# First SwiGLU step: the up half's scale taken with the residual; low parts of 54 weight units by VectorE instead of an accumulating DMA

## The chip, the cores and the metric

The kernel runs on one core of one Trainium2 chip. Its engines are TensorE (PE in the profile, with its weight loads as PEld), VectorE (DVE), ScalarE (ACT), GpSimd (POOL) and SyncE (SP, which here only issues DMAs). The metric is the time of one execution on the device in microseconds (us); the trace and the profile page come from one execution taken with the profiler.

## The reference

A two-layer encoder over 512 tokens of width 1024 (the first layer mixes by S5 and gated linear attention, the second by retention), in float32:

```
for i in range(2):
    x = x + 0.5 * swiglu_ffn(rmsnorm(x, ffn1_norm[i]), ffn1_w1[i], ffn1_w2[i])
    h = rmsnorm(x, mix_norm[i])
    x = x + (s5_gla_mixer(h, ...) if i == 0 else retention_mixer(h, ret_w_in, ret_norm, ret_w_out))
    x = x + 0.5 * swiglu_ffn(rmsnorm(x, ffn2_norm[i]), ffn2_w1[i], ffn2_w2[i])
return rmsnorm(x, final_norm)

def rmsnorm(x, g):   return x * rsqrt(mean(x * x, -1) + 1e-6) * g
def swiglu_ffn(h, w1, w2):
    gate, up = split(h @ w1, 2, axis=-1)          # 2816 columns each
    return (silu(gate) * up) @ w2
```

`retention_mixer` projects h to q, k (8 heads of 128), v (8 heads of 256) and a gate, rotates q and k by cosine and sine tables, forms decayed scores per head, multiplies them with v, normalizes each head, multiplies with silu of the gate and projects back.

## The kernel before

The state x lies transposed in SBUF: 8 tiles of 128 features x 512 tokens. Every product of float32 numbers is made of three matmuls: each operand is split into a high part and a low part (the rest), and `mm3` (L194) adds high x high (L196), high x low (L197) and low x high (L198) in one PSUM bank. A matmul here is 128x128 weights with 512 columns. The norm's division by the root mean square is left out of the operands: rs (L170, one value per token, the same in all partitions) multiplies results instead.

**Weight units.** A unit is 128x1024 numbers, 512 KB, and serves 24 matmuls. `weights` (L175) stages it: SP loads `raw` (4 tiles), ScalarE casts the high part `wh` (L183, 3 tiles of each of `wh` and `wl`), and the low part `wl` comes in one of two ways. With `plain`, VectorE subtracts the high part from `raw` (L185). Without it, `lows` lets ScalarE write -raw, rounded, into `wl` (L191), and a DMA from GpSimd's queue accumulates `raw` into it (L192). The weight loads are given a priority AHEAD (50, 150, 50 by stage, L31), by which a scheduler puts their instructions that much earlier than their place in the program; every engine then works off its own queue in order. PSUM has 7 banks `mm` in a ring: a new product takes the bank that was used seven products before, once what read it is done.

**First FFN** (`ffn`, 0 to 421 us). The first product runs over 22 pairs j, a gate unit and an up unit each. `gate` (L231 on) makes, per pair: t = gate x rs (L232), s = silu(t) (ScalarE, L234), u = up x rs (L236), g = u x s (L238), and splits g into high (ScalarE, L223) and low (VectorE, L224). Behind the pairs j = 5 to 12 the S5 preparation is put in: eight blocks of table work, in which VectorE makes `vt` and `wt` (L626 to L628) and the rotation tables (L718 to L723), GpSimd makes its half of `wt` with the same three lines, TensorE transposes `vt` (L649) and multiplies with `wt` (L662), and ScalarE copies the results (L650, L665). The second product runs over 8 output blocks n of 66 matmuls each, its weights in 22 units, and adds 0.5 x the bank to x[n] (L269), from which the next norm's operands are prepared (`prep`).

**Retention** (1370 to about 1800 us). Four groups g of two heads: four units q, k, q, k (`qk`), four value units over four banks (`values`), two scores of four banks each (`scores`), four gate units (`out_gate`), and `attend` per head. In the first group the values come before the scores, in the others after the first head's scores. `rotated` takes a bank with three multiplies (L1083, L1084, L1085; the last frees it) and an addition (L1086); the cosine and sine tables are loaded in the first group after its first unit (L1105) and scaled by rs (L1106, L1107). `scores` multiplies each bank with the decay (L1129). `attend` ends in L1164, L1165 (VectorE), L1167 (ScalarE) and L1168 (VectorE). Between the first FFN and the retention mixer lie the S5 and attention mixer and two FFNs of another form (`ffn7`, seven products in place of eight); after it follow one more of these and the final norm.

Of the kernel before, what the change touches and what calls it, by code (L numbers as in the profile page):

```python
# [20 lines left out]
ALU = mybir.AluOpType  # L21
# [29 lines left out]
def encoder(tc, I, out, dbg=None):  # L51
    nc = tc.nc
    V, A, G, T = nc.vector, nc.scalar, nc.gpsimd, nc.tensor
# [3 lines left out]
    with ExitStack() as ctx:  # L57
# [9 lines left out]
        x = [xs[:, i] for i in range(KT)]  # L67
# [27 lines left out]
        def tmp(tag, shape=(128, S), dt=F32):  # L95
            return tp.tile(list(shape), dt, name=tag, tag=tag)

        def bank(name="mm"):
            return pp.tile([128, S], F32, name=name, tag="mm")
# [46 lines left out]
        def prep(i, n, acc):  # L146
            if n in SEVEN:
                operand7(i, n)
            else:
                operand(i, n)  # L150
            squares(i, acc)
# [9 lines left out]
        def new_acc():  # L161
            return tp.tile([128, S], F32, name="sumsq", tag="sumsq", bufs=1)

        def rstd(acc):
            st = sp.tile([128, S], F32, name="st", tag="st")
            T.matmul(st, ones, acc, start=True, stop=True)
            sd = tmp("tc")
            A.activation(sd, st, AF.Sqrt, bias=eps, scale=1.0 / D)
            rs = tp.tile([128, S], F32, name="rs", tag="rs", bufs=1)
            V.reciprocal(rs, sd)  # L170
            return rs

        phase = [0]

        def weights(src, plain=False):  # L175

            with tc.high_priority(AHEAD[phase[0]]):
                c = slice(0, src.shape[-1])
                raw = wp.tile([128, 1024], F32, name="raw", tag="raw", bufs=4)
                dma(raw[:, c], src)  # L180
                h = wp.tile([128, 1024], F32R, name="wh", tag="wh")
                l = wp.tile([128, 1024], F32R, name="wl", tag="wl")
                A.copy(h[:, c], raw[:, c])  # L183
                if plain:
                    V.tensor_tensor(l[:, c], raw[:, c], f32(h[:, c]), op=ALU.subtract)  # L185
                else:
                    lows(l[:, c], raw[:, c])
            return h, l

        def lows(l, raw):  # L190
            A.activation(l, raw, AF.Copy, scale=-1.0)  # L191
            G.dma_start(l, raw, accum_op=ALU.add)  # L192

        def mm3(ps, lh, ll, rh, rl, first, last, go_on=False):  # L194

            T.matmul(ps, lh, rh, start=first, stop=False, skip_group_check=go_on)  # L196
            T.matmul(ps, lh, rl, start=False, stop=False, skip_group_check=go_on)  # L197
            T.matmul(ps, ll, rh, start=False, stop=last, skip_group_check=go_on)  # L198

        def project(*srcs, loaded=None):  # L200

            w = loaded or [weights(src) for src in srcs]
            res = [bank() for _ in w]
            for k in range(KT):
                c = slice(k * 128, (k + 1) * 128)
                for ps, (h, l) in zip(res, w):
                    mm3(ps, h[:, c], l[:, c], yh[k], yl[k], k == 0, k == KT - 1)
            return res

        def project_tokens(src):  # L210

            banks = [bank() for _ in range(4)]
            for u in range(4):
                h, l = weights(src[u])
                for k2 in range(2):
                    k, c = u * 2 + k2, slice(k2 * 512, (k2 + 1) * 512)
                    for t in range(4):
                        tt = slice(t * 128, (t + 1) * 128)
                        mm3(banks[t], yh[k][:, tt], yl[k][:, tt], h[:, c], l[:, c], k == 0, k == KT - 1)
            return banks  # L220

        def split(src, hi, lo):
            A.copy(hi, src)  # L223
            V.tensor_tensor(lo, src, f32(hi), op=ALU.subtract)  # L224


        def ffn(w1, w2, acc, nxt, slot, filler=None, loaded=None):
            gh, gl = [], []

            def gate(j, pg, pu, rs):  # L230
                t = tmp("ta")  # L231
                V.tensor_tensor(t, pg, rs, op=ALU.mult)  # L232
                s = tmp("tb")
                A.activation(s, t, AF.Silu)  # L234
                u = tmp("tc")
                V.tensor_tensor(u, pu, rs, op=ALU.mult)  # L236
                g = tmp("ta")
                V.tensor_tensor(g, u, s, op=ALU.mult)  # L238
                h, l = slot(2 * j), slot(2 * j + 1)
                split(g, h, l)  # L240
                gh.append(h)
                gl.append(l)

            first = project(w1[0, 0], w1[0, 1], loaded=loaded)
            for j in range(1, NPAIR):
                pg, pu = (project(w1[j, i])[0] for i in range(2))
                if j == 1:
                    rs = rstd(acc)
                    gate(0, *first, rs)
                gate(j, pg, pu, rs)  # L250
                if filler is not None:
                    filler(j)
            acc = new_acc()
            units = {}

            def second(n, k):

                u, i = divmod(n * NPAIR + k, 8)
                if u not in units:
                    units[u] = weights(w2[u])  # L260
                c = slice(i * 128, (i + 1) * 128)
                h, l = units[u]
                return h[:, c], l[:, c]

            for n in range(KT):
                ps = bank()
                for k in range(NPAIR):
                    mm3(ps, *second(n, k), gh[k], gl[k], k == 0, k == NPAIR - 1)
                V.scalar_tensor_tensor(x[n], ps, 0.5, x[n], op0=ALU.mult, op1=ALU.add)  # L269
                prep(n, nxt, acc)  # L270
            return acc

# [469 lines left out]
        def s5_gla(acc, nxt, mp):  # L742
# [5 lines left out]


            ub = project(W[0], W[1])  # L750
            rs = rstd(acc)
            rq, rk = slot("rq"), slot("rk")
# [268 lines left out]
            for ps in project_tokens(I["ab_v"]):  # L1021
                z = ytile(F32)
                A.copy(z, ps)
                v.append(z)
# [51 lines left out]
        def retention(acc, nxt, mp):  # L1076
            slot = lambda name, dt=F32: mp.tile([128, S], dt, name=name, tag="u", bufs=32)
            W = I["ret_in"]
            rs = None

            def rotated(ps, cos, sin):
                m1, m2 = tmp("ta"), tmp("tb")
                V.tensor_tensor(m1, ps, cos, op=ALU.mult)  # L1083
                V.tensor_tensor(m2[0:64], ps[64:128], sin[64:128], op=ALU.mult)  # L1084
                V.tensor_tensor(m2[64:128], ps[0:64], sin[0:64], op=ALU.mult)  # L1085
                V.tensor_tensor(m1, m1, m2, op=ALU.add)  # L1086
                h, l = slot("rh", F32R), slot("rl", F32R)
                split(m1, h, l)
                return h, l
# [5 lines left out]
            def qk(g):  # L1095
                nonlocal rs
                for h2 in range(2):
                    for w in range(2):
                        ps = project(W[g, h2 * 2 + w])[0]
                        if rs is None:  # L1100
                            rs = rstd(acc)

                            for tab, name in ((ctab, "rcos"), (stab, "rsin")):
                                t = tmp("tc")
                                dma(t, I[name])  # L1105
                                V.tensor_tensor(tab[0], t, rs, op=ALU.mult)  # L1106
                                V.tensor_tensor(tab[1], tab[0], rs, op=ALU.mult)  # L1107
                        (q, k)[w][g * 2 + h2] = rotated(ps, ctab[w], stab[w])
# [23 lines left out]
                    pts[h].append((hi, lo))  # L1132

            def out_gate(g, i):
                ps = project(W[g, 8 + i])[0]
                t = tmp("ta")
                V.tensor_tensor(t, ps, rs, op=ALU.mult)
                z = ytile(F32)
                A.activation(z, t, AF.Silu)
                so[g * 4 + i] = z  # L1140
# [96 lines left out]
        with tc.tile_pool(name="g0a", bufs=14) as ga:  # L1237
# [6 lines left out]
            def filler(j):  # L1244
                if j == 1:
                    dma(ident, I["ident"])
                next(pieces, None)
                if j == 12:
                    for _ in pieces:
                        raise RuntimeError("S5 pieces left")  # L1250
                    wk_pool.__exit__(None, None, None)
                    gb.append(ctx2.enter_context(tc.tile_pool(name="g0b", bufs=18)))
# [10 lines left out]
        w2 = lambda i: (I["w2a"][i], I["w2b"][i])  # L1263
# [158 lines left out]
```

## Time and profile before

| | |
|---|---|
| time, median of 3 runs | 2162.1 us (2160.69 to 2163.96) |
| the profiled execution: its time, its span | 2168.18 us, 2166.4 us |
| TensorE busy, mean granted clock | 2091.4 us (97%), 0.988 of full speed |
| VectorE, ScalarE, GpSimd busy | 1384.0 us, 1144.9 us, 308.7 us |
| high parts cast (L183) | 227 of 1026 ns |
| low parts by ScalarE and DMA (L191, L192) | 221 of each |
| low parts by VectorE (L185) | 72, of 128x1024 and 128x768 |

Section 5 of the page groups instructions by line; its last columns tell how long the engine stood just before them and what ended that. A wait is put down to what came last. Matmuls overlap: one is busy 0.39 us and the next starts 0.23 us after it, so a pause shows as idle time in brackets, with its releaser. The granted clock is given as a share of full speed (2.4 GHz; the other level is 1.2).

### The profile page before, as it was taken

How to read it: one execution, taken by the hardware profiler on the slowest of the kernel's cores; microseconds unless marked ns; L12 is line 12 of the kernel's file. 1: busy time of each engine (PE TensorE's matmuls, PEld its weight loads, DVE VectorE, ACT ScalarE, POOL GpSimd, SP SyncE). 2: the span in 40 equal slices, each digit the busy share in tenths (PEclk: the TensorE clock that was granted, in tenths of full speed). 3: DMA queues.
4: the chain of work that ended last, by engine and by line, in shares of the span. 5: the costliest groups of instructions: out<-in, count | busy, mean ns of one | idle time of the engine just before them, and what ended most of it. 6: DMA issues, size and time to landing. Idle time of an engine off the chain costs nothing.

```text
span 2166.4 us, 31101 instructions
## 1 busy us (share of the span) xinstructions
PE 2091.4 (97%) x12088; PEld 1819.0 (84%) x12088; DVE 1384.0 (64%) x2233; ACT 1144.9 (53%) x1696; POOL 308.7 (14%) x330
## 2 busy tenths in 40 slices
PE   8989999998999999999999999999999998999998
PEld 6877788776888999997989898778888888899997
DVE  7798211059939868578868576454535368868574
ACT  7544444364377555456646364455555566454453
POOL 3432112211012000002000001201111112010001
PEclk9999999998999999999999999999999999999999
DMA  8878888885566463544445352757676754354541
GB/s 233 207 191 224 200 189 191 206 230 164 147 157 160 127 157 127 145 137 117 125 139 166 113 149 100 189 153 177 155 184 150 173 143 126 115 152 132 142 141 49
DMA packets 115860, 340.23 MB, mean 157 GB/s; under 512 B 19040, under 2 KB 33760, under 8 KB 115584
## 3 DMA queue, kind: packets, MB, share of 16 engines
q1 hardware_dynamic: 83888, 222.36, 30.5%
q0 software_dynamic: 31824, 115.88, 28.3%
q8 instruction: 95, 1.56, 0.3%
q14 instruction: 53, 0.43, 0.1%
HBM read 208.18 MB, written 14.14 MB: 103 GB/s over the span
## 4 chain that ended last, share of the span: by engine, by line
PE 55%; DVE 11%; DMA 6%; issue 4%; ACT 3%; SPq 1%; POOL 1%; DVEq 0%; POOLq 0%; ACTq 0%
PE mm L196 18%; PE mm L198 18%; PE mm L197 18%; DMA raw<-in_ffn_w_dram 2%; DMA wl<-raw 1%; DVE s L318 1%; DMA raw<-in_w2b_dram 1%; DVE wl L185 1%; DVE s L312 1%; DVE s L317 1%; DVE s L311 1%; ACT r13h L223 1%; SPq L761 1%; DVE r13l L224 0%; DVE st L956 0%
## 5 line engine op out<-in xcount | busy, mean ns | idle before, releaser
L183 ACT CAST wh<-raw 128x1024 fp32r<-128x1024 f32 (+1 forms) x227 | 232.1, 1026 | 369.0 <-issue 204.2
L192 POOL DMA_DIRECT2D wl<-raw x221 | 190.8, 865 | 1593.4 <-ACT wl L191 1227.8
L196 PE MATMUL mm<-y,wh 128*128 128x512 f32 x776 | 309.7, 399 | 8.0 <-ACT wh L1229 5.0
L198 PE MATMUL mm<-y,wl 128*128 128x512 f32 x776 | 306.6, 395 | 8.6 <-DMA wl<-raw 8.6
L197 PE MATMUL mm<-y,wh 128*128 128x512 f32 x776 | 307.8, 397 | 0.1
L196 PE MATMUL mm<-g,wh 128*128 128x512 f32 (+1 forms) x672 | 259.5, 387 | 4.3 <-ACT g L223 4.3
L197 PE MATMUL mm<-g,wh 128*128 128x512 f32 (+1 forms) x672 | 258.9, 385 | 0.2 <-DVE g L224 0.2
L198 PE MATMUL mm<-g,wl 128*128 128x512 f32 (+1 forms) x672 | 258.9, 385 | 0.0
L191 ACT ACTIVATE wl<-raw 128x1024 fp32r<-128x1024 f32 x221 | 233.1, 1055 | 38.7 <-PE mm L197 23.3
L196 PEld LDWEIGHTS mm<-y,wh 128*128 128x128 f32 x776 | 147.2, 190 | 45.4 <-ACT wh L1229 5.0
L198 PEld LDWEIGHTS mm<-y,wl 128*128 128x128 f32 x776 | 147.1, 190 | 44.4 <-DMA wl<-raw 11.1
L197 PEld LDWEIGHTS mm<-y,wh 128*128 128x128 f32 x776 | 147.3, 190 | 34.4 <-DVE y L106 2.5
L196 PEld LDWEIGHTS mm<-g,wh 128*128 128x128 f32 x672 | 126.5, 188 | 29.2 <-ACT g L223 5.2
L198 PEld LDWEIGHTS mm<-g,wl 128*128 128x128 f32 x672 | 126.7, 188 | 25.7
L197 PEld LDWEIGHTS mm<-g,wh 128*128 128x128 f32 x672 | 126.6, 188 | 25.3 <-DVE g L224 1.1
L398 DVE SCALAR_TENSOR_TENSOR ta<-mm,rs 128x512 f32<-128x512 f32 (+1 forms) x74 | 49.8, 674 | 98.9 <-PE mm L198 98.9
L301 ACT CAST wh<-raw 128x1024 fp32r<-128x1024 f32 x66 | 69.2, 1048 | 65.4 <-PE mm L197 49.3
L159 POOL TENSOR_TENSOR sumsq<-sumsq,tb 128x512 f32<-128x512 f32 x47 | 72.1, 1535 | 205.8 <-ACT tb L158 204.7
L346 ACT COPY sv<-mm 128x256 f32<-128x256 f32 x198 | 72.0, 364 | 43.6 <-PE mm L198 43.0
L185 DVE TENSOR_TENSOR wl<-raw,wh 128x1024 fp32r<-128x1024 f32 (+1 forms) x72 | 81.1, 1129 | 14.6 <-ACT wh L183 14.6
L223 ACT CAST r2h<-s 128x512 fp32r<-128x512 f32 x66 | 41.0, 622 | 92.2 <-DVE s L312 92.1
L389 ACT ACTIVATE tb<-ta 128x512 f32<-128x512 f32 x66 | 41.7, 632 | 84.1 <-DVE ta L388 84.1
(391 smaller groups left out, 5576.6 us busy)
## 6 DMA issues: line engine op xcount, KB each, us to landing
wl<-raw POOLq DMA_DIRECT2D x221, 512.0 KB, 5.4
raw<-in_ffn_w_dram SPq DMA_DIRECT2D x196, 512.0 KB, 3.7
raw<-in_w2b_dram SPq DMA_DIRECT2D x48, 512.0 KB, 3.3
raw<-in_ret_in_dram SPq DMA_DIRECT2D x48, 512.0 KB, 3.6
raw<-in_w2a_dram SPq DMA_DIRECT2D x24, 384.0 KB, 3.0
raw<-in_ret_out_dram SPq DMA_DIRECT2D x16, 512.0 KB, 3.8
raw<-in_ab_in_dram SPq DMA_DIRECT2D x13, 512.0 KB, 5.2
wd<-wt SPq DMA_DIRECT2D x16, 256.0 KB, 2.9
```

The lines of the kernel that those rows point to most:

```text
L159: G.tensor_tensor(acc, acc, sq, op=ALU.add)
L183: A.copy(h[:, c], raw[:, c])
L185: V.tensor_tensor(l[:, c], raw[:, c], f32(h[:, c]), op=ALU.subtract)
L191: A.activation(l, raw, AF.Copy, scale=-1.0)
L192: G.dma_start(l, raw, accum_op=ALU.add)
L196: T.matmul(ps, lh, rh, start=first, stop=False, skip_group_check=go_on)
L197: T.matmul(ps, lh, rl, start=False, stop=False, skip_group_check=go_on)
L198: T.matmul(ps, ll, rh, start=False, stop=last, skip_group_check=go_on)
L223: A.copy(hi, src)
L301: A.copy(h, up)
L346: A.copy(z, ps[:, left])
L398: V.scalar_tensor_tensor(m[:, c], ps[:, c], 0.5, rs[:, c], op0=ALU.mult, op1=ALU.mult)
```

## The change

In `gate` the up bank is multiplied with s directly (L236, now in a tile `tc`), and rs is left to the end: the residual becomes two operations, m = bank x 0.5 x rs and x[n] + m. The low part is made by VectorE (`plain`) for the gate units behind j = 13 (8 units), all 22 units of the second product, and in the retention mixer for the k units, every odd value unit and every odd gate unit (8 of each). The q units, the even ones and all units of the first layer's mixer keep the DMA.

```
-        def project(*srcs, loaded=None):
-            w = loaded or [weights(src) for src in srcs]
+        def project(*srcs, loaded=None, plain=False):
+            w = loaded or [weights(src, plain) for src in srcs]
...
-                h, l = weights(src[u])
+                h, l = weights(src[u], phase[0] == 2 and u % 2 == 1)
...
                 s = tmp("tb")
                 A.activation(s, t, AF.Silu)
-                u = tmp("tc")
-                V.tensor_tensor(u, pu, rs, op=ALU.mult)
-                g = tmp("ta")
-                V.tensor_tensor(g, u, s, op=ALU.mult)
+                g = tmp("tc")
+                V.tensor_tensor(g, pu, s, op=ALU.mult)
...
-                pg, pu = (project(w1[j, i])[0] for i in range(2))
+                pg, pu = (project(w1[j, i], plain=j > 13 and i == 0)[0] for i in range(2))
...
-                    units[u] = weights(w2[u])
+                    units[u] = weights(w2[u], True)
...
-                V.scalar_tensor_tensor(x[n], ps, 0.5, x[n], op0=ALU.mult, op1=ALU.add)
+                m = tmp("ta")
+                V.scalar_tensor_tensor(m, ps, 0.5, rs, op0=ALU.mult, op1=ALU.mult)
+                V.tensor_tensor(x[n], x[n], m, op=ALU.add)
...
-                        ps = project(W[g, h2 * 2 + w])[0]
+                        ps = project(W[g, h2 * 2 + w], plain=w == 1)[0]
...
-                ps = project(W[g, 8 + i])[0]
+                ps = project(W[g, 8 + i], plain=i % 2 == 1)[0]
```

The scheduler orders the queues anew, so instructions move that the diff does not name. The numbers behind the names below count buffers; they differ between the two kernels for the same buffer.

GpSimd's queue in the first FFN, early in the S5 preparation; wl_590 of the kernel before and wl_582 of the changed one are the same unit's low part. Before:

```order
L192 DMA wl_494<-raw_491 128x1024
L192 DMA wl_526<-raw_523 128x1024
L192 DMA wl_590<-raw_587 128x1024
L626 TENSOR_TENSOR wa0_180<-pw0_479,par_327 128x576
L627 TENSOR_TENSOR wa1_181<-pw1_480,par_327 128x576
L628 TENSOR_TENSOR wt1_574<-wa0_180,wa1_181 128x576
L626 TENSOR_TENSOR wa0_180<-pw0_479,par_327 128x576
```

The same place now:

```order
L192 DMA wl_488<-raw_485 128x1024
L192 DMA wl_520<-raw_517 128x1024
L626 TENSOR_TENSOR wa0_180<-pw0_473,par_323 128x576
L627 TENSOR_TENSOR wa1_181<-pw1_474,par_323 128x576
L628 TENSOR_TENSOR wt1_566<-wa0_180,wa1_181 128x576
L192 DMA wl_582<-raw_579 128x1024
L626 TENSOR_TENSOR wa0_180<-pw0_473,par_323 128x576
```

The three table operations moved ahead of that unit's DMA.

ScalarE's queue between the seventh and the eighth S5 block (g is the pair's product, vs the block's table). Before:

```order
L183 CAST wh_1847<-raw_1845 128x1024
L191 ACTIVATE wl_1848<-raw_1845 128x1024
L650 COPY vs_1657<-mm_1661 128x4x128
L223 CAST g_1653<-ta_1651 128x512
L650 COPY vs_1657<-mm_1671 128x4x128
```

The same place now:

```order
L183 CAST wh_1821<-raw_1819 128x1024
L191 ACTIVATE wl_1822<-raw_1819 128x1024
L223 CAST g_1629<-tc_1627 128x512
L650 COPY vs_1633<-mm_1637 128x4x128
L650 COPY vs_1633<-mm_1647 128x4x128
```

L223 moved ahead of both copies.

ScalarE's queue at the end of the first group's second head in the retention mixer (oh are its outputs, wh_14040 and wh_13975 the last k unit of the second group, wh_14128 and wh_14062 its first value unit). Before:

```order
L183 CAST wh_14040<-raw_14038 128x1024
L191 ACTIVATE wl_14041<-raw_14038 128x1024
L1167 ACTIVATE oh_13901<-ta_13898,columns_78 128x512
L183 CAST wh_14128<-raw_14126 128x1024
L1167 ACTIVATE oh_13908<-ta_13905,columns_78 128x512
L191 ACTIVATE wl_14129<-raw_14126 128x1024
```

The same place now:

```order
L183 CAST wh_13975<-raw_13973 128x1024
L183 CAST wh_14062<-raw_14060 128x1024
L1167 ACTIVATE oh_13837<-ta_13834,columns_78 128x512
L191 ACTIVATE wl_14063<-raw_14060 128x1024
L1167 ACTIVATE oh_13844<-ta_13841,columns_78 128x512
```

The value unit's cast moved ahead of the first L1167. VectorE's queue a little later, where the second group's rotations end and its first scores are multiplied with the decay. Before:

```order
L1083 TENSOR_TENSOR ta_14070<-mm_14045,y_13253 128x512
L224 TENSOR_TENSOR rl_14035<-ta_14028,rh_14034 128x512
L1084 TENSOR_TENSOR tb_14071<-mm_14045,y_13255 64x512
L1085 TENSOR_TENSOR tb_14071<-mm_14045,y_13255 64x512
L1129 TENSOR_TENSOR tc_14086<-mm_14082,decay_14080 128x512
L1086 TENSOR_TENSOR ta_14070<-ta_14070,tb_14071 128x512
```

The same place now:

```order
L1084 TENSOR_TENSOR tb_14005<-mm_13979,y_13197 64x512
L1085 TENSOR_TENSOR tb_14005<-mm_13979,y_13197 64x512
L224 TENSOR_TENSOR rl_13970<-ta_13963,rh_13969 128x512
L1086 TENSOR_TENSOR ta_14004<-ta_14004,tb_14005 128x512
L185 TENSOR_TENSOR wl_14094<-raw_14091,wh_14093 128x1024
L1129 TENSOR_TENSOR tc_14020<-mm_14016,decay_14014 128x512
```

The first L1129 moved behind L1086 and a new L185.

## Rows read from the trace of the kernel before

**Rows 1.** The page, part 1: busy us, share of the span, instructions.

```profile
PE 2091.4 (97%) x12088; PEld 1819.0 (84%) x12088; DVE 1384.0 (64%) x2233; ACT 1144.9 (53%) x1696; POOL 308.7 (14%) x330
```

**Rows 2.** Busy us by stretch: PE, PEld, DVE, ACT, POOL; clock, DMA share, GB/s.

```profile
100.00:150.00 50.00, 46.62 (x237) 38.37 (x236) 47.10 (x108) 24.03 (x48) 21.39 (x18) 1.00 0.83 214
150.00:200.00 50.00, 42.08 (x206) 34.01 (x205) 47.04 (x62) 20.76 (x44) 14.23 (x11) 0.97 0.69 190
...
250.00:300.00 50.00, 50.00 (x220) 41.02 (x219) 11.76 (x17) 22.71 (x27) 7.74 (x9) 1.00 0.82 191
```

**Rows 3.** TensorE's waits, 0 to 205 us: total, times, longest.

```profile
PE mm L662 <- DVE wt L628: 7.4, 4, 2.3
...
PE mm L649 <- DVE vt L628: 3.9, 3, 1.5
```

**Rows 4.** TensorE's waits, 205 to 420 us.

```profile
PE mm L198 <- DMA wl<-raw: 1.2, 1, 1.2
```

**Rows 5.** TensorE's waits, 1370 to 1480 us.

```profile
PE mm L197 <- DMA wl<-raw: 1.7, 2, 1.1
PE mm L196 <- DVE tb L1085: 0.9, 1, 0.9
```

**Rows 6.** Lines L185 (ns least/median/most, first and last start) and L192, whole execution.

```profile
L185 DVE TENSOR_TENSOR wl<-raw,wh x72: 940/1216/1227, 716.6 to 2137.9; 128x1024 fp32r<-128x1024 f32 x48, 128x768 fp32r<-128x768 f32 x24
...
DMA to landing us min/median/max: 4.4/5.4/9.7
```

**Rows 7.** Timeline of VectorE, S5 blocks: start, us, instruction, idle before.

```profile
188.67 0.68 DVE L236 TENSOR_TENSOR tc<-mm,rs 128x512 f32<-128x512 f32 x1
189.27 0.67 DVE L628 TENSOR_TENSOR vt<-u,u 128x512 f32<-128x512 f32 x1
...
193.67 0.69 DVE L224 TENSOR_TENSOR g<-ta,g 128x512 fp32r<-128x512 f32 x1 [1.91 <-ACT g L223]
```

**Rows 8.** Timeline of ScalarE before the last S5 block.

```profile
192.53 0.59 ACT L650 COPY vs<-mm 128x512 f32<-128x512 f32 x1 [7.29 <-DMA rd<-rot]
```

**Rows 9.** Timeline of GpSimd, early S5 preparation.

```profile
51.92 0.86 POOL L192 DMA_DIRECT2D wl<-raw  x1 [4.64 <-DVE u L601]
...
57.41 1.77 POOL L628 TENSOR_TENSOR wt<-wa,wa 128x576 f32<-128x576 f32 x1
```

**Rows 10.** Timeline of TensorE, first matmuls with two units' low parts.

```profile
61.04 0.39 PE L198 MATMUL mm<-y,wl 128*128 128x512 f32 x1
...
67.62 0.50 PE L198 MATMUL mm<-y,wl 128*128 128x512 f32 x1 [0.92 <-DMA wl<-raw]
```

**Rows 11.** Timeline of VectorE and SP, start of the retention mixer.

```profile
1371.68 3.35 DVE L170 RECIPROCAL rs<-tc 128x512 f32<-128x512 f32 x1 [6.14 <-ACT tc L168]
...
1385.30 0.69 DVE L1106 TENSOR_TENSOR y<-tc,rs 128x512 f32<-128x512 f32 x1 [3.76 <-DMA tc<-in_rsin_dram]
...
1377.02 0.43 SPq L1105 DMA_DIRECT2D tc<-in_rsin_dram  x1
```

**Rows 12.** Timeline of ScalarE, VectorE, TensorE, second group of the retention mixer.

```profile
1462.51 1.05 ACT L183 CAST wh<-raw 128x1024 fp32r<-128x1024 f32 x1 [1.50 <-PE mm L197]
...
1465.00 0.68 DVE L1085 TENSOR_TENSOR tb<-mm,y 64x512 f32<-64x512 f32 x1
...
1473.73 0.69 DVE L1083 TENSOR_TENSOR ta<-mm,y 128x512 f32<-128x512 f32 x1 [0.51 <-PE mm L198]
...
1476.45 0.69 DVE L1129 TENSOR_TENSOR tc<-mm,decay 128x512 f32<-128x512 f32 x1
...
1478.38 0.39 PE L196 MATMUL mm<-wh,y 128*128 128x512 f32 x1
```

**Rows 13.** Third group: VectorE by stretch (span, busy), timelines of VectorE and TensorE.

```profile
1567.50:1582.33 14.83, 12.66 (x20) 1.00 0.75 175
...
1582.33 0.69 DVE L1129 TENSOR_TENSOR tc<-mm,decay 128x512 f32<-128x512 f32 x1
...
1584.85 0.39 PE L196 MATMUL mm<-wh,y 128*128 128x512 f32 x1
```

## The prediction

> **What bounds the kernel now.** I read the page first: TensorE is busy 97% of the span [rows 1], so only its pauses, and stretches at the lower of its two clock levels (2.4 and 1.2 GHz), can be won or added. The table of busy times by stretch comes second: from 250 to 300 us, in the second product of the first FFN, TensorE has no pause and VectorE 38 us of 50 free, while from 100 to 200 us VectorE is busy 47 of 50 and TensorE stands [rows 2]. Third come TensorE's waits: up to 205 us it waits 7.4 + 3.9 = 11.3 us for `wt` and `vt` (L628, VectorE's part of the S5 tables) [rows 3]; at 216.8 us 1.2 us for a low part that comes by DMA [rows 4]; and from 1370 to 1480 us 1.7 us for two such DMAs and 0.9 us for the bank that L1085 frees [rows 5]. The other pauses lie in stages that the change leaves alone.
>
> **The change part by part.** Every row is from the profiled execution, 2168.18 us, which is 6.1 above the median of the three timed runs; I sum against it and carry the sum to the median.
>
> *Low parts by VectorE.* 54 weight units lose one ScalarE operation (L191) and one accumulating DMA (L192) and gain one subtraction (L185), 1.217 us for 128x1024 [rows 6]. The 22 units of the second product and the 8 gate units behind j = 13 fall where TensorE has no pause and VectorE is three quarters idle [rows 2]: 0, and the residual's extra operation too (one of some 0.7 us per output block, after which TensorE works off 66 matmuls of 0.23 us, 15 us, before the next block's result is due). If that cover were gone, it would be 54 x 1.2 = 65 us; nothing in those stages comes near.
>
> *S5 blocks, 112 to 200 us.* VectorE is the late one. In each of the five pairs of this stretch the two products L236 and L238 become one; the next operation starts 0.60 us after L236 (188.67 to 189.27) [rows 7]: 5 x 0.60 = 3.0 us. Before the last block VectorE also stands 1.91 us for ScalarE's L223 [rows 7], which in ScalarE's queue stands behind an L650 that waited 7.29 us for a DMA [rows 8]; now L223 stands ahead of that L650, so 1.9 us go too. TensorE's restart after the last block moves 4.9 us forward. What is late next is TensorE itself, and that only once all 11.3 us are gone. Bounds: 0 (the DMA of the rotation, not VectorE, is last) and -11.3; I take -4.9, since both parts stand in VectorE's own rows.
>
> *A new wait at 61 us.* On GpSimd one L192 now stands behind L626, L627 and L628. Before, it was issued at 51.92, and the last of the three ran until 57.41 + 1.77 = 59.18 [rows 9]. They wait for ScalarE's copies, ahead of which one operation of about 1 us (L191 of the same unit) is gone, so they end at about 58.1. With the landing of 4.4, 5.4 or 9.7 us (least, median, most [rows 6]) the low part is there at 62.5, 63.5 or 67.8; TensorE asks for it at 61.04 [rows 10], and waits 1.5, 2.5 or 6.8. Behind L192 in GpSimd's queue stand the next L626 and L627 and then the next unit's L192; that unit's own pause, 0.92 us at 67.62 [rows 10], goes, since TensorE comes later. Net +0.5, +1.5 or +5.8; I take the median, +1.5. It passes on: the S5 blocks start from TensorE's products.
>
> Here a rule speaks against the change. The granted clock was 1.00 over 100 to 150 us, which hold a pause of 2.3, and 0.97 over 150 to 200, which hold the shorter ones that follow each other closely [rows 2, 3]: 3% of 50 us is 1.5 us of full-speed work lost. The Trainium skill ("TensorE: Matmul & The Clock Gate", Part 1) says that the array falls to 1.2 GHz when it idles and comes back after sustained work. By that the new pause could cost its own length and another 1.5 us. By the row at 145 us a single pause of this length cost no clock; the sum follows the row, the range holds the 1.5.
>
> *The pause at 216.8 us.* This unit's low part still comes by DMA, but the neighbour's transfer of 512 KB goes: between -1.2 (all) and +1 (the same bytes at another moment); I take -0.5.
>
> *Start of the retention mixer.* VectorE waits for the sine table until 1385.30 [rows 11]. Its DMA was issued at 1377.02, behind weight loads on SP's queue that waited for staging tiles held by accumulating DMAs of q and k units. The two k units now free theirs after a subtraction. The tile for the table is free after L170, at 1371.68 + 3.35 = 1375.03 [rows 11], so it can be issued some 2 us sooner and meets fewer transfers (it took 8.3 us). The bank of q0 then comes before TensorE asks, and so do the two late low parts, whose casts stood behind the rotated q: 1.7 + 0.9 [rows 5] and 0.1 for each of three restarts (0.50 in place of 0.39 us [rows 10]) = 2.9. Bounds -2.9 and 0; I take -2.9.
>
> *Retention, second group.* In ScalarE's queue the cast of a value unit, which waits for TensorE until 1462.51, now stands ahead of both L1167; the first of them comes at about 1463.5, after which VectorE has L1168, L1083, L1084 and L1168 again to do, and L1085 starts at 1467.0 instead of 1465.00 [rows 12]: 2.0 late. Ahead of the first L1129 the new L185 (1.1 to 1.2 us) and L1086 (0.6) are put in: 3.75, less 0.51 of idle time in between [rows 12], 3.2. L1129 frees the bank of the first scores for the fourth value bank: before it ended at 1476.45 + 0.69 = 1477.14, and TensorE asked at 1478.38 [rows 12], 1.24 later. So TensorE stands 2.0 us. Groups three and four have the same insertions, but more room: 14.83 - 12.66 = 2.2 us idle in VectorE, and 1584.85 - 1583.02 = 1.8 us [rows 13]: 3.8 - 2.2 - 1.8 = 0. Upper bound: no idle time absorbs anything and two L185 fall in: 2.05 + 2.4 - 1.24 = 3.2 in group two and 2.05 + 2.4 - 1.83 = 2.6 in each of the others, 8.4 in all. Lower bound 0. I take +2.0.
>
> *Sum:* -4.9 + 1.5 - 0.5 - 2.9 + 2.0 = **-4.8 us**: 2163.4 in an execution like the profiled one, **2157.3** at the median.
>
> **The rivals.**
> *More gain:* ScalarE's cast costs the second group nothing, because VectorE's queue has slack that I did not see, and the landing at 61 us is a quick one: -4.8 - 2.0 - 1.0 = -7.8, 2154.3. For it: a third of VectorE's time in these groups is free. Against: each operation named stands in one queue in this order.
> *A gain missing:* the S5 blocks are held by the DMA of the rotation or the sine table stays late, so the change does there not what its queues promise: without the 2.9, -1.9; without the 4.9, +0.1; about 2161. For it: both chains contain a DMA whose landing varies by 2 to 5 us.
> *Slower, by one mechanism:* VectorE's queue in the retention mixer becomes the bound. A subtraction there waits for its cast, which waits for TensorE to leave a weight tile; all behind it, L1085 and L1129 first, free banks late. Price: 8.4 in the three groups, and at the start, where a subtraction stands behind the sine table, the 2.9 is not won: -4.8 + 2.9 - 2.0 + 8.4 = +4.5, 2166.6. It decides from the point where the first L1129 of groups three and four starts more than 1.8 us later against the values' matmuls than before. For it: the same three rows of order in every group. Against: the idle 2.2 us.
> *The clock rule* of the new wait: with a pause of 2.5 us and half clock behind it, -4.8 + 1.5 = -3.3, 2158.8.
>
> **How the numbers follow.** What a measurement can tell from no change is about 0.2%, 4.3 us. The sum 0.42 (its own range 2154.5 to 2160, straddling the 4.3: faster 0.25, same 0.17); more gain 0.20 (faster); a gain missing 0.16 (same); slower 0.15 (0.14 slower, 0.01 same); the clock rule 0.07 (0.02 faster, 0.05 same). Together faster 0.47, same 0.39, slower 0.14. The range reaches from below the second case, 2152, to the slower one, 2166.
>
> **What would show it.** Right: VectorE's pause before the last S5 block gone and TensorE's waits for L628 down from 11.3 to about 6.5; one pause of about 2.5 us at 61 us for a low part; no wait for L1085 at 1388; in the second group one pause of about 2 us, ended by L1129, and none in the next two. Wrong: pauses ended by L1129 in all groups, waits ended by L185, a late sine table, or pauses in the second product, where I count none.

## The result, and the profile after

The changed kernel takes 2154.26 us (median of 6, 2148.64 to 2154.95), the kernel before beside it 2163.37 (6, 2160.69 to 2170.34); the ratio is 0.9942, interval 0.9925 to 0.9958, or -12.5 us (-16.2 to -9.1). The two medians differ by 9.1 us, which is the near end of that interval. The forecast was -4.8: right in sign, and too small by half or more. The profiled execution took 2154.95 us with a span of 2153.0.

The page, part 1, of after answers to [rows 1], and two of its groups show the 54 units that changed hands: L185, 72 before, is now 126 and busy 66.7 us more (147.8 against 81.1; counted: 65). VectorE as a whole has 60.2 us more, since the scale's edit takes 14 shorter operations out on balance.

```profile
PE 2092.0 (97%) x12088; PEld 1820.5 (85%) x12088; DVE 1444.2 (67%) x2273; ACT 1095.6 (51%) x1642; POOL 255.0 (12%) x276
...
L192 POOL DMA_DIRECT2D wl<-raw x167 | 143.5, 859 | 1494.4 <-ACT wl L191 1148.9
...
L185 DVE TENSOR_TENSOR wl<-raw,wh 128x1024 fp32r<-128x1024 f32 (+1 forms) x126 | 147.8, 1175 | 113.1 <-ACT wh L183 108.7
```

The table by stretch [rows 2] says where TensorE gained early on: 150 to 200 us, busy 45.8 us in place of 42.1. In the second product (250 to 300) it is busy throughout, as before, beside a VectorE with 5 us more to do.

```profile
100.00:150.00 50.00, 47.77 (x240) 39.27 (x238) 46.80 (x107) 24.52 (x49) 18.70 (x17) 0.97 0.82 206
150.00:200.00 50.00, 45.78 (x224) 37.51 (x223) 49.00 (x61) 21.15 (x45) 14.46 (x12) 0.97 0.79 218
250.00:300.00 50.00, 50.00 (x220) 41.04 (x219) 16.59 (x20) 17.17 (x21) 2.56 (x3) 1.00 0.52 143
```

TensorE's waits up to 205 us [rows 3]: the 11.3 us for L628 are 5.8, with 0.6 for a cast beside them.

```profile
PE mm L662 <- DVE wt L628: 5.2, 3, 1.9
...
PE mm L649 <- DVE vt L628: 0.6, 1, 0.6
PE mm L649 <- ACT wh L183: 0.6, 1, 0.6
```

VectorE before the last S5 block [rows 7]: the split of `g` (L224) has no idle time in front of it.

```profile
190.05 0.68 DVE L627 TENSOR_TENSOR u<-pv,par 128x512 f32<-128x512 f32 x1
190.66 0.68 DVE L224 TENSOR_TENSOR g<-tc,g 128x512 fp32r<-128x512 f32 x1
```

GpSimd and TensorE around 61 us [rows 9, 10]: L192 stands behind L628 and is issued at 57.91; the low part lands about 5.0 us later, and TensorE waits 1.43.

```profile
56.19 1.77 POOL L628 TENSOR_TENSOR wt<-wa,wa 128x576 f32<-128x576 f32 x1
57.91 0.88 POOL L192 DMA_DIRECT2D wl<-raw  x1
...
62.94 0.50 PE L198 MATMUL mm<-y,wl 128*128 128x512 f32 x1 [1.43 <-DMA wl<-raw]
```

VectorE and SP at the start of the retention mixer [rows 11]: the sine table is issued 3.4 us after the start of the reciprocal, where it was 5.3 (1377.02 against 1371.68).

```profile
1364.04 3.35 DVE L170 RECIPROCAL rs<-tc 128x512 f32<-128x512 f32 x1 [0.78 <-ACT tc L168]
...
1367.42 0.33 SPq L1105 DMA_DIRECT2D tc<-in_rsin_dram  x1
```

Of TensorE's waits from 1350 to 1480 us [rows 5] all that is left is:

```profile
PE mm L196 <- DVE tc L1129: 0.2, 1, 0.2
```

Lined up by the same matmul (its start in the one trace against its start in the other), TensorE is 5.7 us ahead of before at 428 us and gains 3.4 at the start of the retention mixer. It loses about 2.5 between 428 and 1007 us, and gains 2.6 (1007 to 1099 us of before), 0.9 (1293 to 1362) and 4.6 (behind 1480) in FFNs whose code the diff does not touch. Those last three no step of the forecast has; but the 4.6 is no larger than what a second execution of the kernel before gains there by itself (below).

### The profile page after: what moved, and what is told of

Same layout as the page of the kernel before. It is cut to its first block, busy times and chain, and to the rows that moved or that the text cites. A ratio compares the mean times of both kernels' runs of the same rounds, so it can differ in the third digit from the quotient of the medians.

```text
span 2153.0 us, 30985 instructions
## 1 busy us (share of the span) xinstructions
PE 2092.0 (97%) x12088; PEld 1820.5 (85%) x12088; DVE 1444.2 (67%) x2273; ACT 1095.6 (51%) x1642; POOL 255.0 (12%) x276
## 3 DMA queue, kind: packets, MB, share of 16 engines
q8 instruction: 95, 1.56, 0.3%
## 4 chain that ended last, share of the span: by engine, by line
PE 77%; DVE 12%; DMA 4%; ACT 3%; issue 3%; POOL 1%; SPq 0%; DVEq 0%; POOLq 0%; ACTq 0%
PE mm L196 25%; PE mm L198 25%; PE mm L197 25%; DMA raw<-in_ffn_w_dram 2%; DMA wl<-raw 1%; DVE wl L185 1%; POOL sumsq L159 1%; DVE s L318 0%; DVE st L956 0%; PE mm L662 0%; DVE s L312 0%; DMA raw<-in_w2b_dram 0%; DVE st L954 0%; ACT wl L191 0%; DVE s L317 0%
## 5 line engine op out<-in xcount | busy, mean ns | idle before, releaser
L192 POOL DMA_DIRECT2D wl<-raw x167 | 143.5, 859 | 1494.4 <-ACT wl L191 1148.9
L185 DVE TENSOR_TENSOR wl<-raw,wh 128x1024 fp32r<-128x1024 f32 (+1 forms) x126 | 147.8, 1175 | 113.1 <-ACT wh L183 108.7
L191 ACT ACTIVATE wl<-raw 128x1024 fp32r<-128x1024 f32 x167 | 176.1, 1055 | 27.6 <-DMA raw<-in_ab_in_dram 16.2
L196 PEld LDWEIGHTS mm<-y,wh 128*128 128x128 f32 x776 | 147.8, 191 | 46.1 <-ACT wh L1229 5.9
L301 ACT CAST wh<-raw 128x1024 fp32r<-128x1024 f32 x66 | 69.2, 1049 | 57.9 <-PE mm L197 49.5
L224 DVE TENSOR_TENSOR r13l<-s,r13h 128x1024 fp32r<-128x1024 f32 x66 | 81.6, 1237 | 9.6 <-ACT r13h L223 9.6
L223 ACT CAST r2h<-s 128x512 fp32r<-128x512 f32 x66 | 41.0, 621 | 88.8 <-DVE s L312 88.6
```

What stands on the lines that cost most here:

```text
L301: A.copy(h, up)
```

## The experiments

Three runs do one part each, beside one look at the kernel before. Each ratio is to runs of before on the same chip in the same series, with its 95% interval in brackets; at 2167 us 0.001 is 2.2 us.

**The kernel before once more.**

> The kernel before once more, for a second trace. In the first pair of traces the changed kernel gains 9.4 us up to the second group of the retention mixer and another 4.6 us behind it, where no instruction of the two queues differs. Theory A (that late gain is only the spread between executions): the second trace of the kernel before takes 2 to 5 us less behind 1480 us than the first one did, and its total lies near 2163. Theory B (fewer accumulating DMAs help everywhere): its late part is as long as in the first trace, within 1 us.

One execution, 2178.53 us, longer than each of the 24 timed runs of before in this series. Theory A's total is a miss, its late part is not: lined up with the first trace by the same matmul, this one loses 8.8 us between 428 and 680 us, and from 1480 to 2100 us it is 4.4 us quicker, with no change in the kernel. So the changed kernel's 4.6 behind 1480 us, read against the first trace alone, is no evidence for the change by itself. Other readings differ too: TensorE waits 6.4 + 2.5 = 8.9 us for L628 where the first trace has 11.3, the wait for L1085 at the start of the retention mixer is absent, and the clock over 100 to 150 us is 0.98 where it was 1.00:

```profile
PE mm L662 <- DVE wt L628: 6.4, 4, 2.3
...
PE mm L649 <- DVE vt L628: 2.5, 2, 1.4
...
100.00:150.00 50.00, 46.60 (x241) 38.47 (x239) 46.82 (x110) 26.08 (x51) 19.29 (x16) 0.98 0.85 212
```

**Scale and residual alone.** All low parts as before. Of the diff only the residual in two operations and, cut from it:

```diff
-                u = tmp("tc")
-                V.tensor_tensor(u, pu, rs, op=ALU.mult)
-                g = tmp("ta")
-                V.tensor_tensor(g, u, s, op=ALU.mult)
+                g = tmp("tc")
+                V.tensor_tensor(g, pu, s, op=ALU.mult)
```

> Only the scale moved to the residual (one multiplication fewer per pair, one operation more per output block); all low parts as before. Theory A (the parts add, each in its own stage): 4 to 6 us faster, all before 220 us: the pause at 67.6 us gives way to one of about 1.4 us at 61 us, TensorE's waits for L628 fall from 11.3 to about 6 us, and the pause at 216.8 us stays or shrinks. Rival C (the S5 blocks wait for the rotation's DMA, not for VectorE): no change within 1 us.

2164.12 us (12 runs) against 2166.99 (24): 0.9986 (0.9972 to 1.0), -3.0 us, with no gain at the end of the interval. The forecast's terms for it are -4.9 + 1.5 = -3.4; the -0.5 at 216.8 us hangs on a neighbour's low part and belongs to the next run (here that pause stays).

**The first FFN's low parts alone.**

```diff
-                pg, pu = (project(w1[j, i])[0] for i in range(2))
+                pg, pu = (project(w1[j, i], plain=j > 13 and i == 0)[0] for i in range(2))
-                    units[u] = weights(w2[u])
+                    units[u] = weights(w2[u], True)
```

> Only the 8 gate units behind j = 13 and the 22 units of the second product with VectorE's subtraction; scale and retention as before. Theory A: 0 to -2 us, since TensorE has no pause in these stages; at most the 1.2 us at 216.8 go, if the neighbour's accumulating DMA was the cause. Theory B (less DMA traffic makes all landings quicker): 3 to 5 us faster, spread over the stages that follow too.

2159.59 us (7 runs): 0.9967 (0.9954 to 0.998), -7.2 us where the forecast has 0 for these units and -0.5 for the pause at 216.8 us. It is more than either theory had put. This is the step that failed.

**The retention mixer's low parts alone.**

```diff
-                        ps = project(W[g, h2 * 2 + w])[0]
+                        ps = project(W[g, h2 * 2 + w], plain=w == 1)[0]
```

(with the same for L214 and L1135).

> Only the retention mixer's 24 units with VectorE's subtraction; the first FFN as before. Theory A: 2.5 to 3.5 us faster, all between 1370 and 1410 us (no wait for L1085 and no late low parts there), less a pause of 0.2 to 0.5 us ended by L1129 in the second group; nothing behind it. Theory B: 6 us or more, with a gain of over 2 us behind 1480 us. The prediction's own step (a pause of 2.0 us in the second group): only about 1 us faster.

2165.46 us (12 runs): 0.9985 (0.9969 to 1.0), -3.3 us, again with no gain at the end of the interval. The three parts add to -0.62%, the whole change has -0.58%.

**Where the first FFN's part gains.** Hardly in the first FFN: from 205 to 300 us TensorE waits once before, the 1.2 us at 216.8, and not at all with the part. It gains in the FFNs of another form behind 800 us, whose code is the same: lined up with the first trace of before, it loses 2.6 us up to 800 us and is 11.0 quicker from there to 2150 (4.1 of these, at 1858 to 1900 us, the second trace of before has too). The marker is TensorE's wait for L359, VectorE's difference of two products. From 800 to 2150 us (total, times, longest), the kernel before first, then the first FFN's part:

```profile
PE mm L196 <- DVE ta L359: 5.8, 7, 1.3
```

```profile
PE mm L196 <- DVE ta L359: 1.3, 2, 0.8
```

Those near 1063, 1300 and 1967 us are among the ones that go. Followed back from 1300, ScalarE's waits over 1250 to 1302 us of before hold one for weights to cast (L301), which over the same stretch with the first FFN's part is missing:

```profile
ACT wh L301 <- DMA raw<-in_ffn_w_dram: 2.8, 4, 1.6
```

Those weights are late because SP's load (L290) waited for a staging tile that an accumulating DMA held. The transfers while one such DMA is in flight (issued at 1235.33 by before, at 1236.01 with the part), as 40 slices of GB/s and by queue (packets, MB, share of 16 engines); before first:

```profile
GB/s 0 0 0 0 0 0 0 0 0 139 389 0 389 28 361 56 361 56 333 83 333 111 278 167 250 194 0 28 0 28 0 28 0 28 0 28 0 0 0 0
...
q0 software_dynamic: 144, 0.52, 45.2%
q8 instruction: 1, 0.02, 1.6%
```

```profile
GB/s 0 0 0 0 0 0 0 0 0 0 0 0 0 39 505 78 194 349 78 272 311 39 272 311 39 272 349 0 272 349 0 311 311 0 388 233 0 0 0 0
...
q0 software_dynamic: 143, 0.52, 63.0%
...
wl<-raw POOLq DMA_DIRECT2D x1, 512.0 KB, 4.6
```

SP's next load, before and then with the part:

```profile
1241.30 0.33 SPq L290 DMA_DIRECT2D raw<-in_ffn_w_dram  x1
```

```profile
1240.64 0.33 SPq L290 DMA_DIRECT2D raw<-in_ffn_w_dram  x1
```

In before one packet of the instruction queue q8 (16 KB, 1.5 us on one of the 16 DMA engines) falls into the transfer. The transfer is nearly over when a tail of 28 GB/s follows: five packets of 4 KB one after the other, 0.31 us apart, with nothing else of it left. I read it as one engine still working off what stood behind the instructions; the trace does not name the engine. It lands after 5.9 us, in the other kernel after 4.6. L290 comes at 1241.30 - 1235.33 = 5.97 us after the issue instead of 4.63. The Trainium skill ("Runtime: NRT & Kernel Launch", Instruction fetch mechanics) says that an engine's instructions are fetched in blocks of 16 KiB, 256 instructions, and that the cost of crossing a block's boundary is mostly hidden. The block agrees (the page of before has `q8 instruction: 95, 1.56`: 95 packets, 1.56 MB, for 24326 instructions of TensorE's stream, 256 each). TensorE itself stands nowhere from 1205 to 1260 us; the transfer beside the packet lands late.

Why would the packet move? A unit whose low part comes by VectorE needs fewer waits in TensorE's stream: counted in the trace, 147 wait instructions before, 131 with the first FFN's part, 122 in the changed kernel. So theory F (F for fetch): the change moves the later fetches off the accumulating transfers. Its rival, theory B: fewer accumulating transfers (30 fewer here) are a gain in themselves. A third reason, a new order of the queues, is ruled out by the next runs: read from the traces, all five engines do the same instructions in the same order with and without the idle ones at the head.

**Sixteen instructions more.** Into the kernel with the first FFN's part, at the head of TensorE's queue, into a PSUM tile that is overwritten later:

```diff
+        pad = sp.tile([128, S], F32, name="st", tag="st")
+        for _ in range(4):
+            T.matmul(pad[:, 0:1], ones, ones[:, 0:1], start=True, stop=True)
```

> The low parts of the 8 gate units and the 22 units of the second product by VectorE, as in the run of that part alone, and four small float32 products of one column at the head of TensorE's queue, where TensorE waits for its first data. They add about 16 instructions to TensorE's stream and nothing else. Theory F (where the 16 KB packets of TensorE's instruction queue fall among the accumulating transfers decides the late gain): the fetches come again at the places of the kernel before, the pauses of VectorE's product at L362 come back near 1063, 1300 and 1967 us, and the ratio to the kernel before is 0.9985 (0.997 to 1.000), 3 to 7 us above the run of that part alone. Theory B (fewer accumulating transfers are the gain in themselves): nothing changes, ratio 0.9967 (0.995 to 0.998), no such pause.

2167.52 us (12 runs) against 2167.21 (24): 0.9996 (0.9984 to 1.0008). No gain is left (3.5 us at the far end of the interval), by sixteen instructions that run while TensorE waits for its first data; the waits for the product (now L362, from 800 to 2150 us) are back:

```profile
PE mm L199 <- DVE ta L362: 5.3, 7, 1.2
```

Theory B cannot be the whole reason. The medians differ by 7.9 us; in the two profiled executions these waits account for 4.0. The one with the sixteen is the quickest of its twelve (2161.79): lined up, its first 800 us happen to be 6.8 us quicker than without them, and the stretch from 800 to 2150 us takes 8.0 longer.

**A whole packet more.** If the position counts, 256 instructions must do nothing where 16 did all:

```diff
+        pb = ones.bitcast(mybir.dt.bfloat16)
+        for _ in range(128):
+            T.matmul(pad[:, 0:1], pb[:, 0:128], pb[:, 0:1], start=True, stop=True)
```

> The low parts of the 8 gate units and the 22 units of the second product by VectorE, and at the head of TensorE's queue 128 bfloat16 products of one column: 256 instructions, one whole packet of its stream. Theory F: every later fetch falls at the same product as without them, so the seven-fold pause of VectorE's product (at L359 before, L363 here) stays at two times and about 1.3 us behind 800 us, with none near 1063, 1300 or 1967 us of the program without the head; against the kernel before the ratio is 0.9967 plus what of the head lies on the path (128 times 0.06 to 0.2 us are 8 to 26 us, some 4 us of them in the wait for the first data and some given back as the loads run ahead: 0.997 to 1.004). Theory P (any products at the head bring the pauses back, whatever their number): seven such pauses, 5 us or more, as with the sixteen.

2159.94 us (12 runs) against 2166.26 (33): 0.9971 (0.9957 to 0.9985), the gain kept. The head cost next to nothing (128 products in 3.6 us, all in the wait for the first data, where I had put 8 to 26). The page has one packet more,

```profile
q8 instruction: 96, 1.57, 0.3%
```

and the waits for the product (L363 here, 800 to 2150 us) are at two places again:

```profile
PE mm L200 <- DVE ta L363: 1.9, 2, 1.3
```

**The kernel before with 240 more,** sixteen short of a packet, all transfers as before. First with sixty float32 products:

> The kernel before with sixty small float32 products of one column at the head of TensorE's queue, about 240 instructions, which is 16 short of one packet of 256. The arithmetic and all transfers are those of before. Theory F: each fetch falls about 16 instructions later in the program, as it did with the low parts of the first step by VectorE; the pauses near 1063, 1300 and 1967 us go, ratio 0.9975 (0.996 to 0.999), though the first SwiGLU step keeps its pauses. Theory B: ratio 1.000, with the products of the head in TensorE's wait for its first data, or above 1 if they reach past it (sixty times about 0.1 to 0.25 us are 6 to 15 us, and the first product of before starts behind them).

2174.13 us (9 runs): 1.004 (1.0023 to 1.0057), a miss. The head took 25.8 us, for which I had put 6 to 15, and TensorE's first real product came at 26.69 in place of 4.99. Then with 120 in bfloat16:

> The kernel before with 120 bfloat16 products of one column at the head of TensorE's queue: 240 instructions, sixteen short of a packet, in place of the sixty float32 ones whose head cost more than it gave back. Theory F: the pauses near 1300 and 1967 us of before stay away, as with the float32 head, and the time behind the first 300 us is 4 to 8 us less than before; in all 0.9965 to 1.002, by what the head costs. Theory B: the time behind the first 300 us is that of before.

2163.43 us (12 runs): 0.9981 (0.9961 to 1.0), -4.1 us, inside what theory F gave (0.9965 to 1.002), though the interval just reaches no gain. TensorE starts at 5.09, and the waits near 1300 and 1967 us are gone, as in the float32 run; the one near 1063 stays. So a kernel that differs from before by idle products alone has, by its median ratio, about half of the first FFN part's gain. Its waits for the product:

```profile
PE mm L200 <- DVE ta L363: 4.1, 4, 1.4
```

**The changed kernel with 16, 64 and 128 more** (4 float32, 32 and 64 bfloat16 products).

> The changed kernel with the four small products at the head of TensorE's queue. Theory F: it loses part of what it won behind 800 us, ratio to the kernel before 0.9965 (0.995 to 0.9985), some 3 to 6 us above the changed kernel, with pauses at L359's place near 1063 or 1300 us. Theory B: the same as the changed kernel, ratio 0.9942 (0.9925 to 0.996).

> The changed kernel with 32 bfloat16 products of one column at the head, 64 instructions, a quarter of a packet. The head costs 0 to 3 us (32 times 0.06 to 0.2 us, some 4 us of it in the wait for the first data). Theory F: the pauses behind 800 us are others than in the changed kernel and with sixteen instructions, and the time is anywhere within 8 us above or 4 us below the changed kernel's. Theory B: the changed kernel's time plus the head, with its pauses near 946, 1861 and 2077 us and no others.

> The changed kernel with 64 bfloat16 products of one column at the head, 128 instructions, half a packet; the head costs 0 to 9 us by the same working. Theory F: again other pauses behind 800 us, the time within 8 us above or 4 us below the changed kernel's, apart from the head. Theory B: the changed kernel's time plus the head, with its pauses.

2159.43, 2158.03 and 2156.48 us: 0.9964 (0.9946 to 0.9982), 0.9962 (0.9946 to 0.9978) and 0.9951 (0.9934 to 0.9967), against 0.9942 without. The first has a median 5.2 us above the changed kernel's, but its runs of before were slower too: by medians against their own series the two have 0.9964 and 0.9958, and the intervals overlap, so a loss of time is not shown. Theory F shows in its seven waits for the product again:

```profile
PE mm L199 <- DVE ta L362: 5.3, 7, 1.4
```

The other two differ from it as well (a wait near 1858 of 1.7 us with 64; one near 1056 of 1.9 with 128, the place that is 1063 in before); that they are slower than the changed kernel is not shown.

All fourteen traces at the place at 1235 us, read from their records: us from the issue of that L192 to the start of the instruction packet, and to the landing; last, whether TensorE waits for the product near 1300 us.

```
fetch 1.4 to 2.1 us behind the issue: before, its second run, scale alone,
  retention alone, first FFN + 16, changed + 16      landing 5.8 to 6.4; wait in all 6
fetch 4.1 to 4.4 behind it: first FFN alone, + 256, changed, changed with
  more units, before + 240 (both)                    landing 4.4 to 4.7; wait in none of 6
no fetch within: changed + 64, changed + 128         landing 4.4; wait in none of 2
```

Retention alone, whose stream is the same up to 1350 us, has the late landing here; at 1967 us, behind its own shorter stream, its wait is missing. The same two groups part in time: from 800 to 2150 us, lined up with the first trace of before and less what the start of the retention mixer gives where its low parts are changed (2.6 to 2.9 us), the five other traces with a late landing here are -0.2 to 3.9 us quicker than it, the eight with an early one 4.5 to 11.0.

**More units of the changed kernel by VectorE,** where low parts still pause TensorE (61, 417 and 434.6 us):

```diff
-                pg, pu = (project(w1[j, i], plain=j > 13 and i == 0)[0] for i in range(2))
+                pg, pu = (project(w1[j, i], plain=(j > 13 or j == 4) and i == 0)[0] for i in range(2))
-            ub = project(W[0], W[1])
+            ub = project(W[0], W[1], loaded=[weights(W[0]), weights(W[1], True)])
-                to_chunks(j, project(W[j])[0])
+                to_chunks(j, project(W[j], plain=j == 3)[0])
```

> The changed kernel, with the low part by VectorE also for the gate unit whose landing pauses TensorE at 61 us and for two units of the first mixer whose landings pause it at 417 and 434.6 us. By the pauses of the changed kernel (1.4, 0.6 and 3.5 us) it is up to 5.5 us quicker, 2149 us (ratio to before 0.9917, 0.990 to 0.994), if VectorE and ScalarE hold no other wait there. Theory F adds that TensorE's stream loses some three instructions more, so the places of the later fetches move by three products and the late stages may give some of it back, up to 3 us. Theory B: the full gain.

2156.58 us (6 runs): 0.9943 (0.9924 to 0.9961), the same as the changed kernel and short of what I had put (0.990 to 0.994). The pauses moved: from 405 to 500 us the changed kernel waits 4.1 + 3.0 us, this one 10.8:

```profile
PE mm L198 <- DMA wl<-raw: 4.1, 2, 3.5
PE mm L197 <- DMA wl<-raw: 3.0, 1, 3.0
```

```profile
PE mm L197 <- DMA wl<-raw: 7.8, 2, 4.2
PE mm L196 <- ACT wh L183: 2.0, 1, 2.0
PE mm L198 <- DMA wl<-raw: 1.0, 1, 1.0
```

No version here beats the changed kernel.

## Why the prediction was wrong in size, point by point

*"The 22 units of the second product and the 8 gate units ... 0".* This step failed: -7.2 us (-10.0 to -4.3) by the run of that part alone, the pause at 216.8 us included. The cover held (no wait from 205 to 300 us, none ended by L185), but the sum knew only the stages that the edit touches. "The other pauses lie in stages that the change leaves alone" was taken to mean that they stay. That was the mistake: TensorE's program became shorter by wait instructions, its fetches fell elsewhere, and transfers of FFNs far behind, as the one read at 1235 us, ran without them. Sixteen idle instructions undo it, 256 do not. That the late landing at 1235 us leads to the wait at 1300 rests on the waits read above and on both coming and going together in 14 traces; not every link between them was followed. Nor is the whole gain divided among such places: those near 1063, 1300 and 1967 us are the ones read. Not settled either: sixteen instructions are 1.0 to 1.8 us of TensorE's stream there (16 of 256, with 29.0 us in before from the packet ahead and 16.4 to the next), and the packet moved by 2.7.

*S5 blocks, -4.9.* Right in mechanism, about 1 to 2 us too large: both parts are as read (one operation less in each pair, and no 1.91 us ahead of the split). The waits for L628 went from 11.3 to 5.8 us, but the second trace of before has 8.9. Lined up from 100 to 205 us, TensorE gained 3.8 against the first trace, 3.0 against the second, and 3.7 in the run of the scale alone.

*New wait at 61 us, +1.5.* Right in place and cause, too large: L192 was issued at 57.91 as worked out (58.1), and the landing took 5.0 instead of the median 5.4, so 1.43 us of waiting; without the 0.92 of the next unit it is about +0.5, the lower of the three values named. The clock was 1.00 over the 40 us behind it in this trace, so this pause cost no clock. It was 0.97 over 100 to 150 us, where before had 1.00 [rows 2], though the pauses there are shorter; the second trace of before has 0.98, so this need not be the change.

*The pause at 216.8, -0.5.* It is gone entirely, -1.2 and with the restart -1.7: the far bound, and a little more.

*Start of the retention mixer, -2.9.* Right: no wait is left, and TensorE gained 3.4 against the first trace, 2.7 against the second.

*Second group, +2.0.* Half right. VectorE's queue is late as foretold: L1129 starts at 1469.73, 3.4 us behind the start of the values' matmuls (1466.35), while before it started 0.2 behind it (1476.45 against 1476.28). But TensorE waits 0.22. TensorE's own order moved too, which the forecast did not weigh: the fourth value bank's first matmul, the one that needs L1129, is the seventeenth of the values (1470.46, 4.1 us in) and no longer the tenth (1478.38, 2.1 us in) [rows 12].

```profile
1466.35 0.40 PE L196 MATMUL mm<-wh,y 128*128 128x512 f32 x1
...
1469.73 0.68 DVE L1129 TENSOR_TENSOR tc<-mm,decay 128x512 f32<-128x512 f32 x1
...
1470.46 0.50 PE L196 MATMUL mm<-wh,y 128*128 128x512 f32 x1 [0.22 <-DVE tc L1129]
```

Groups three and four have no pause, as said. With this term at +0.2 the retention part is -2.7 in place of -0.9; alone it measured -3.3 (-6.7 to 0), an interval that holds both.

*The rivals.* "More gain" named this group and the quick landing, and both came true, but its 2154.3 meets the measured median by another cause: the two are worth 1.8 and 1.0 us here, the first FFN's part 7. That the total came near this rival is luck. The one on the slower side did not occur; VectorE's queue is late in the groups, and TensorE's order leaves room for it.

## What to carry to other kernels

An edit can move the time in stages that it does not touch, here because the number of instructions in an engine's stream sets when its program is fetched. Before a gain or loss of a few tenths of a per cent is put down to an edit, add a handful of idle instructions at the head of that engine's queue, and a whole block as the control. Take a second trace of the kernel before, too: two executions of it differ by 4 us in a stretch where one might look for the edit. And a wait worked out from one engine's new order has to be checked against the new order of the engine that is to wait.

## What the runs showed of the hardware that I had not expected

One 16 KB instruction packet, of 0.9 to 1.9 us, goes with a landing 1.2 to 2 us later of a 512 KB accumulating transfer at 1235 us. In the table above the delay is there whenever the packet starts within 2.1 us of the issue, and not once when it starts 4.1 behind it. Over whole traces it is smaller and not always there: of the accumulating transfers in all fourteen that had no other data transfer beside them in their first 4.4 us, 287 without an instruction packet beside them landed in 4.35 to 5.17 us (median 4.40), 33 with one within 2.2 us of the issue in 4.40 to 5.92 (median 5.2), and 11 with one at least 4.0 us behind it in 4.38 to 4.66.

A matmul of one column took 0.21 us in float32 (each product is two of them in the trace: 120 for sixty products, in 25.8 us) and 0.03 in bfloat16 (128 in 3.6).

With waits of 3.6 and 4.2 us that end at 482.6 and 494.6 the kernel with more units had a granted clock of 0.67 over 480 to 500 us, so much of that stretch was at 1.2 GHz, and the changed kernel, with one of 3.0 there, 0.91. Over 530 to 550 us the first had 0.57 with a wait of only 1.0 ahead of it, the second 0.83 with one of 3.0 that ends at 532.9 and two shorter ones ahead of it (1.3 and 0.9), which I cannot explain. Columns: span and busy us by engine (count), clock, DMA share, GB/s; the kernel with more units first.

```profile
480.00:500.00 20.00, 13.19 (x37) 10.16 (x38) 19.80 (x27) 9.93 (x15) 2.58 (x3) 0.67 0.73 178
530.00:550.00 20.00, 19.34 (x112) 18.45 (x113) 18.30 (x42) 1.08 (x3) 0.93 (x3) 0.57 0.48 147
```

```profile
480.00:500.00 20.00, 16.96 (x82) 13.87 (x81) 19.71 (x29) 12.17 (x21) 2.15 (x6) 0.91 0.39 109
530.00:550.00 20.00, 17.14 (x148) 15.73 (x148) 17.31 (x41) 8.33 (x12) 3.27 (x9) 0.83 0.86 260
```
